# Softmax-minus-one-hot over 8192 x 8192 logits: six in-place f32 row buffers, a row maximum, one compare-and-subtract pass, labels loaded once

## The chip, the cores and the metric

One core of one Trainium2 chip runs the program. The metric is device time in microseconds (us); lower is better. Most executions of one kernel agree within 0.3%. The profile also gives a span, from the first to the last instruction of the program on the core, which is here about 2 us shorter than the time.

In the profile DVE is VectorE, ACT is ScalarE, POOL is GpSimd, PE is TensorE, and SP is the engine that here only issues loads. "ACTq" and "SPq" are the sequencers of ACT and SP issuing a DMA. L85 is line 85 of the kernel.

## The reference

```python
batch, seq_len, vocab = 8, 1024, 8192          # logits f32, labels int
logits_max = np.max(logits, axis=-1, keepdims=True)
exp_logits = np.exp(logits - logits_max)
softmax = exp_logits / np.sum(exp_logits, axis=-1, keepdims=True)
one_hot = ...                                  # 1.0 at the label of each row
return (softmax - one_hot).astype(np.float32)
```

Seen from the chip it is 8192 rows of 8192 f32: 268.44 MB must be read and 268.44 MB written. The kernels cut it into 64 tiles of 128 rows, 4 MB each.

## The kernel before

Each tile is loaded by SP, exponentiated by ACT into bf16 (with the row sum as a by-product and no maximum subtracted), finished by three DVE passes, and stored by ACT's queue. Four row buffers (`bufs=4`) are shared by loading, computing and storing. The labels of each tile come by a small load of their own on POOL's queue.

```python
io_pool = ctx.enter_context(tc.tile_pool(name="io", bufs=4))
work_pool = ctx.enter_context(tc.tile_pool(name="work", bufs=2))
...
for ti in range(n_tiles):
    rs = ti * P
    logits_tile = io_pool.tile([P, V], fp32, tag="io")
    nc.sync.dma_start(out=logits_tile[:], in_=logits_nv[rs : rs + P, :])
    labels_tile = stats_pool.tile([P, 1], labels_n.dtype, tag="labels")
    nc.gpsimd.dma_start(out=labels_tile[:], in_=labels_n[rs : rs + P, None])
    ...                                             # cast of the labels to f32
    nc.scalar.activation(out=exp_bf[:], in_=logits_tile[:], func=Exp, ..., accum_out=sum_f32[:])
    nc.vector.reciprocal(out=recip_sum[:], in_=sum_f32[:])
    ohts_bf = logits_tile.bitcast(bf16)[:, :V]
    nc.vector.tensor_scalar(out=ohts_bf, in0=iota_pv[:, :], scalar1=labels_f32[:],
                            scalar2=sum_f32[:], op0=is_equal, op1=mult)          # L74
    nc.vector.tensor_sub(out=exp_bf[:], in0=exp_bf[:], in1=ohts_bf)              # L83
    nc.vector.tensor_scalar_mul(out=logits_tile[:], in0=exp_bf[:], scalar1=recip_sum[:])  # L85
    nc.scalar.dma_start(out=out_nv[rs : rs + P, :], in_=logits_tile[:])          # L87
```

The softmax here doesn't subtract the row's maximum and nothing guards it: scores larger than these inputs give would overflow.

## Time and profile before

| | before |
|---|---|
| time | 1255.14 us (median of 3, 1254.55 to 1255.56) |
| span of the profiled run | 1252.6 us |
| DMA rate, 200 to 1200 us | 433 GB/s at DMA share 1.00 |
| DVE, ACT busy | 58%, 36% |
| period of a tile in the middle | 19.4 us |

The head of the page of the kernel before, with its DMA part. "q1" carries the loads, "q10" the stores, "q0" the small label loads; the share is the time that their packets took, of 16 engines' span:

```profile
span 1252.6 us, 992 instructions
DVE 732.6 (58%) x320; ACT 457.0 (36%) x129; POOL 253.0 (20%) x69
...
q1 hardware_dynamic: 9216, 268.44, 49.8%
q10 hardware_dynamic: 9216, 268.44, 49.6%
q0 software_dynamic: 2048, 0.07, 0.1%
```

The two large queues together fill 99.4% of the DMA engines' time. No compute engine is near that. The kernel is bound by the DMA engines, and the question for any change is what it does to them.

The table of stretches of the kernel before (columns: stretch, its length, busy us and instructions of DVE, ACT and POOL, PE clock, DMA share, GB/s). A packet is booked in whole where it falls, so short stretches can show a little over 1.00:

```profile
800.00:1000.00 200.00, 118.61 (x53) 73.00 (x22) 42.84 (x10) 1.00 1.00 433
...
1228.00:1232.00 4.00, 2.94 (x3) 1.00 (x2) 0.00 (x0) 1.00 1.08 467
1232.00:1236.00 4.00, 3.99 (x1) 0.00 (x0) 0.00 (x0) 1.00 0.51 221
1236.00:1240.00 4.00, 3.98 (x1) 0.00 (x0) 0.00 (x0) 1.00 0.00 0
1240.00:1244.00 4.00, 0.51 (x1) 0.00 (x0) 0.00 (x0) 1.00 0.92 393
```

In the middle, with transfers cut and issued as they are here, there is nothing to gain short of moving fewer bytes. At the end the DMA engines run dry for several us and then start once more. The timeline of the kernel before shows why (start, length, what):

```profile
1221.87 7.03 ACT L61 ACTIVATE exp_bf<-logits_tile 128x8192 bf16<-128x8192 f32 x1 [12.24 <-DMA logits_tile<-in_logits_dram]
1221.92 0.34 ACTq L87 DMA_DIRECT2D out_dram<-logits_tile  x1
...
1229.11 2.41 DVE L74 TENSOR_SCALAR logits_tile<-iota_pv,labels_f,sum_f 128x8192 bf16<-128x8192 int16 x1
1231.56 4.43 DVE L83 TENSOR_TENSOR exp_bf<-exp_bf,logits_tile 128x8192 bf16<-128x8192 bf16 x1
1236.02 4.49 DVE L85 TENSOR_SCALAR logits_tile<-exp_bf,recip_sum 128x8192 f32<-128x8192 bf16 x1
1240.54 0.34 ACTq L87 DMA_DIRECT2D out_dram<-logits_tile  x1
```

The last load lands at 1221.87. The last store is issued 18.7 us later, but what was still queued for storing lasted only about 12 us.

The time to landing of the large transfers, from the DMA part of the page (columns: count, KB each, median us):

```profile
logits_tile<-in_logits_dram SPq DMA_DIRECT2D x64, 4096.0 KB, 27.2
out_dram<-logits_tile ACTq DMA_DIRECT2D x64, 4096.0 KB, 31.3
```

Read it as an account of buffers: a buffer spends 27.2 us loading, about 19 in compute and 31.3 storing, 77.5 us in all, which is four periods of 19.4. Four buffers are all in use, all the time.

### The profile page before, as it was taken

How to read it: one execution, taken by the hardware profiler on the slowest of the kernel's cores; microseconds unless marked ns; L12 is line 12 of the kernel's file. 1: busy time of each engine (PE TensorE's matmuls, PEld its weight loads, DVE VectorE, ACT ScalarE, POOL GpSimd, SP SyncE). 2: the span in 40 equal slices, each digit the busy share in tenths (PEclk: the TensorE clock that was granted, in tenths of full speed). 3: DMA queues.
4: the chain of work that ended last, by engine and by line, in shares of the span. 5: the costliest groups of instructions: out<-in, count | busy, mean ns of one | idle time of the engine just before them, and what ended most of it. 6: DMA issues, size and time to landing. Idle time of an engine off the chain costs nothing.

```text
span 1252.6 us, 992 instructions
## 1 busy us (share of the span) xinstructions
DVE 732.6 (58%) x320; ACT 457.0 (36%) x129; POOL 253.0 (20%) x69
## 2 busy tenths in 40 slices
DVE  3764655746647556465574664755646556465573
ACT  4424244243342433423424334243342432423422
POOL 5322212212122122221221212212222122100000
DMA  9999999999999999999999999999999999999997
GB/s 400 421 435 434 433 428 430 433 436 433 435 430 432 431 433 433 434 434 432 429 432 435 431 434 433 431 432 432 434 433 434 433 429 432 432 434 435 434 433 311
DMA packets 20487, 537.01 MB, mean 429 GB/s; under 512 B 4096, under 2 KB 4096, under 8 KB 4096
## 3 DMA queue, kind: packets, MB, share of 16 engines
q1 hardware_dynamic: 9216, 268.44, 49.8%
q10 hardware_dynamic: 9216, 268.44, 49.6%
q0 software_dynamic: 2048, 0.07, 0.1%
q14 instruction: 7, 0.06, 0.0%
HBM read 268.50 MB, written 268.44 MB: 429 GB/s over the span
## 4 chain that ended last, share of the span: by engine, by line
DMA 71%; DVE 17%; issue 8%; ACT 1%; POOL 1%; ACTq 0%; SPq 0%; PEldq 0%
DMA out_dram<-logits_tile 38%; DMA logits_tile<-in_logits_dram 32%; DVE logits_tile L85 7%; DVE exp_bf L83 7%; DVE logits_tile L74 4%; ACT exp_bf L61 1%; DMA labels_tile<-in_labels_dram 1%; POOL iota_pv L41 1%; ACTq L87 0%; POOL labels_tile L50 0%; DVE labels_f L57 0%; DVE recip_sum L71 0%; SPq L47 0%; ACTq L61 0%; PEldq L113 0%
## 5 line engine op out<-in xcount | busy, mean ns | idle before, releaser
L61 ACT ACTIVATE exp_bf<-logits_tile 128x8192 bf16<-128x8192 f32 x64 | 449.8, 7029 | 771.3 <-DMA logits_tile<-in_logits_dram 757.8
L50 POOL DMA_DIRECT2D labels_tile<-in_labels_dram x64 | 245.9, 3843 | 832.1 <-DVE labels_f L57 830.1
L71 DVE RECIPROCAL recip_sum<-sum_f 128x1 f32<-128x1 f32 x64 | 10.5, 163 | 485.1 <-ACT exp_bf L61 485.1
L85 DVE TENSOR_SCALAR logits_tile<-exp_bf,recip_sum 128x8192 f32<-128x8192 bf16 x64 | 287.1, 4486 | 0.1
L83 DVE TENSOR_TENSOR exp_bf<-exp_bf,logits_tile 128x8192 bf16<-128x8192 bf16 x64 | 283.2, 4425 | 2.2
L74 DVE TENSOR_SCALAR logits_tile<-iota_pv,labels_f,sum_f 128x8192 bf16<-128x8192 int16 x64 | 154.3, 2412 | 0.3 <-issue 0.3
L57 DVE CAST labels_f<-labels_tile 128x1 f32<-128x1 int32 x64 | 9.4, 147 | 20.2 <-DMA labels_tile<-in_labels_dram 20.2
L61 ACT ACTIVATION_READ_ACCUMULATOR exp_bf<-logits_tile 128x1 f32 x64 | 11.9, 186 | 0.0
L41 POOL IOTA iota_pv<- 128x8192 int16 x1 | 6.9, 6944 | 0.4 <-PEq L113 0.4
L61 ACT ACT_TABLE_LOAD x1 | 1.3, 1283 | 0.7 <-PEq L102 0.7
L102 POOL MEMSET const-float32-0.0<- 128x1 f32 x1 | 0.1, 99 | 0.2 <-issue 0.2
L102 POOL MEMSET const-bfloat16-1.0<- 128x1 bf16 x1 | 0.1, 102 | 0.0
L102 POOL MEMSET const-uint8-127<- 128x1 uint8 x1 | 0.1, 102 | 0.0
L102 POOL MEMSET const-float32-1.0<- 128x1 f32 x1 | 0.1, 99 | 0.0
## 6 DMA issues: line engine op xcount, KB each, us to landing
logits_tile<-in_logits_dram SPq DMA_DIRECT2D x64, 4096.0 KB, 27.2
out_dram<-logits_tile ACTq DMA_DIRECT2D x64, 4096.0 KB, 31.3
labels_tile<-in_labels_dram POOLq DMA_DIRECT2D x64, 1.0 KB, 12.7
```

Of the source, the lines that this page charges most:

```text
L41: nc.gpsimd.iota(iota_pv[:, :], [[1, V]], channel_multiplier=0)
L50: nc.gpsimd.dma_start(out=labels_tile[:], in_=labels_n[rs : rs + P, None])
L57: nc.vector.tensor_copy(out=labels_f32[:], in_=labels_i32)
L61: nc.scalar.activation(out=exp_bf[:], in_=logits_tile[:], func=mybir.ActivationFunctionType.Exp, bias=0.0, scale=1.0, accum_out=sum_f32[:],)
L71: nc.vector.reciprocal(out=recip_sum[:], in_=sum_f32[:])
L74: nc.vector.tensor_scalar(out=ohts_bf, in0=iota_pv[:, :], scalar1=labels_f32[:], scalar2=sum_f32[:], op0=mybir.AluOpType.is_equal, op1=myb ...
L83: nc.vector.tensor_sub(out=exp_bf[:], in0=exp_bf[:], in1=ohts_bf)
L85: nc.vector.tensor_scalar_mul(out=logits_tile[:], in0=exp_bf[:], scalar1=recip_sum[:])
L102: nc = _bacc.Bacc("TRN2", target_bir_lowering=False, num_devices=1)
```

## The change

The intent is exactness (the maximum is subtracted and everything stays f32) without a price. The data stay in place in one f32 buffer per tile, which frees the bf16 buffers and gives six row buffers instead of four. DVE finds the row maximum of tile t+1 while ACT normalizes tile t; one DVE pass per half row compares an index row with the label and subtracts. The labels are loaded once, transposed on PE, and kept. The instructions stay in the order in which they are written.

```diff
-    io_pool = ctx.enter_context(tc.tile_pool(name="io", bufs=4))
-    work_pool = ctx.enter_context(tc.tile_pool(name="work", bufs=2))
+    io = ctx.enter_context(tc.tile_pool(name="io", bufs=SLOTS))      # SLOTS = 6, HALF = 4096
+    ctx.enter_context(tc.manual_schedule())
...
-        nc.gpsimd.dma_start(out=labels_tile[:], in_=labels_n[rs : rs + P, None])
+    nc.scalar.dma_start(out=lab_raw[:], in_=lab_tp)                  # once; then PE transpose
...
+    def row_max(x):
+        nc.vector.tensor_reduce(out=m[:], in_=x[:], axis=X, op=Alu.max, negate=True)
+    def exponent(x, m):
+        nc.scalar.activation(out=x[:], in_=x[:], func=Act.Exp, bias=m[:], scale=1.0, accum_out=s[:])
+    def normalize(x, r):        # two halves
+            nc.scalar.activation(out=xc, in_=xc, func=Act.Copy, bias=0.0, scale=r[:])
+    def subtract(t, x):         # two halves
+            nc.vector.scalar_tensor_tensor(out=xc, in0=iota[:], scalar=lab[:, c, t : t + 1], in1=xc,
+                op0=Alu.is_equal, op1=Alu.subtract, reverse1=True)
...
+    for t in range(T):
+        s = exponent(xs[t], ms[t])
+        r = inverse(s)
+        if t + 1 < T:
+            xs[t + 1] = load(t + 1)
+            ms[t + 1] = row_max(xs[t + 1])
+        if t > 0:
+            store(t - 1, xs[t - 1])
+        normalize(xs[t], r)
+        subtract(t, xs[t])
+    store(T - 1, xs[T - 1])
```

More of the change, by code (lines that the diff above doesn't have):

```diff
@@ L5 @@
 import concourse.tile as tile
-from concourse import bass_utils, mybir
+from concourse import mybir
 from concourse._compat import with_exitstack
 P = 128
+HALF = 4096
+SLOTS = 6
 @with_exitstack
@@ L21 @@
     fp32 = mybir.dt.float32
-    bf16 = mybir.dt.bfloat16
+    i32 = mybir.dt.int32
     i16 = mybir.dt.int16
-    logits_nv = logits.flatten_outer_dims()
-    out_nv = out.flatten_outer_dims()
-    labels_n = labels
-    while len(labels_n.shape) > 1:
-        labels_n = labels_n.rearrange("a b ... -> (a b) ...")
-    N, V = logits_nv.shape
-    assert N % P == 0, f"N={N} must be a multiple of {P}"
-    n_tiles = N // P
-    const_pool = ctx.enter_context(tc.tile_pool(name="const", bufs=1))
-    io_pool = ctx.enter_context(tc.tile_pool(name="io", bufs=4))
@@ L37 @@
-    work_pool = ctx.enter_context(tc.tile_pool(name="work", bufs=2))
-    stats_pool = ctx.enter_context(tc.tile_pool(name="stats", bufs=4))
-    iota_pv = const_pool.tile([P, V], i16)
-    nc.gpsimd.iota(iota_pv[:, :], [[1, V]], channel_multiplier=0)
-    for ti in range(n_tiles):
-        rs = ti * P
-        logits_tile = io_pool.tile([P, V], fp32, tag="io")
-        nc.sync.dma_start(out=logits_tile[:], in_=logits_nv[rs : rs + P, :])
-        labels_tile = stats_pool.tile([P, 1], labels_n.dtype, tag="labels")
-        nc.gpsimd.dma_start(out=labels_tile[:], in_=labels_n[rs : rs + P, None])
-        labels_f32 = stats_pool.tile([P, 1], fp32, tag="labels_f32")
-        if mybir.dt.size(labels_n.dtype) == 8:
-            labels_i32 = labels_tile.bitcast(mybir.dt.int32)[:, :1]
-        else:
-            labels_i32 = labels_tile[:]
-        nc.vector.tensor_copy(out=labels_f32[:], in_=labels_i32)
-        exp_bf = work_pool.tile([P, V], bf16, tag="exp")
-        sum_f32 = stats_pool.tile([P, 1], fp32, tag="sum")
-        nc.scalar.activation(
-            out=exp_bf[:],
-            in_=logits_tile[:],
-            func=mybir.ActivationFunctionType.Exp,
-            bias=0.0,
-            scale=1.0,
-            accum_out=sum_f32[:],
-        )
-        recip_sum = stats_pool.tile([P, 1], fp32, tag="recip")
-        nc.vector.reciprocal(out=recip_sum[:], in_=sum_f32[:])
-        ohts_bf = logits_tile.bitcast(bf16)[:, :V]
-        nc.vector.tensor_scalar(
-            out=ohts_bf,
-            in0=iota_pv[:, :],
-            scalar1=labels_f32[:],
-            scalar2=sum_f32[:],
-            op0=mybir.AluOpType.is_equal,
-            op1=mybir.AluOpType.mult,
-        )
-        nc.vector.tensor_sub(out=exp_bf[:], in0=exp_bf[:], in1=ohts_bf)
-        nc.vector.tensor_scalar_mul(out=logits_tile[:], in0=exp_bf[:], scalar1=recip_sum[:])
-        nc.scalar.dma_start(out=out_nv[rs : rs + P, :], in_=logits_tile[:])
@@ new lines @@
+    Act = mybir.ActivationFunctionType
+    Alu = mybir.AluOpType
+    x_nv = logits.flatten_outer_dims()
+    o_nv = out.flatten_outer_dims()
+    N, V = x_nv.shape
+    T = N // P
+    C = V // HALF
+    lab_tp = labels.rearrange("a b -> (a b)").rearrange("(t p) -> t p", p=P)
+    const = ctx.enter_context(tc.tile_pool(name="const", bufs=1))
+    io = ctx.enter_context(tc.tile_pool(name="io", bufs=SLOTS))
+    stats = ctx.enter_context(tc.tile_pool(name="stats", bufs=4))
+    psum = ctx.enter_context(tc.tile_pool(name="psum", bufs=1, space=bass.MemoryType.PSUM))
@@ new lines @@
+    ctx.enter_context(tc.manual_schedule())
+    lab_raw = const.tile([T, P], labels.dtype)
+    nc.scalar.dma_start(out=lab_raw[:], in_=lab_tp)
+    iota = const.tile([P, HALF], i16)
+    nc.gpsimd.iota(iota[:], [[1, HALF]], base=0, channel_multiplier=0)
+    ident = const.tile([T, T], fp32)
+    nc.gpsimd.memset(ident[:], 0.0)
+    nc.gpsimd.affine_select(
+        out=ident[:], in_=ident[:], compare_op=Alu.not_equal, fill=1.0,
+        base=0, pattern=[[-1, T]], channel_multiplier=1,
+    )
@@ new lines, with load @@
+    lab_f = const.tile([T, P], fp32)
+    lab32 = lab_raw[:].bitcast(i32)
+    step = mybir.dt.size(labels.dtype) // 4
+    nc.vector.tensor_copy(out=lab_f[:], in_=lab32.rearrange("t (p s) -> t p s", s=step)[:, :, 0])
+    lab_ps = psum.tile([P, T], fp32)
+    nc.tensor.transpose(out=lab_ps[:], in_=lab_f[:], identity=ident[:])
+    lab = const.tile([P, C, T], fp32)
+    for c in range(C):
+        nc.vector.tensor_scalar_add(out=lab[:, c, :], in0=lab_ps[:], scalar1=float(-c * HALF))
+    def load(t):
+        x = io.tile([P, V], fp32, tag="x", name="x")
+        nc.sync.dma_start(out=x[:], in_=x_nv[t * P : (t + 1) * P, :])
+        return x
@@ new lines, in row_max, with inverse @@
+    def row_max(x):
+        m = stats.tile([P, 1], fp32, tag="m", name="m")
+        nc.vector.tensor_reduce(out=m[:], in_=x[:], axis=mybir.AxisListType.X, op=Alu.max, negate=True)
+        return m
+    def exponent(x, m):
+        s = stats.tile([P, 1], fp32, tag="s", name="s")
+        nc.scalar.activation(out=x[:], in_=x[:], func=Act.Exp, bias=m[:], scale=1.0, accum_out=s[:])
+        return s
+    def inverse(s):
+        r = stats.tile([P, 1], fp32, tag="r", name="r")
+        nc.vector.reciprocal(out=r[:], in_=s[:])
+        return r
@@ new lines, in normalize, with store @@
+    def normalize(x, r):
+        for c in range(C):
+            xc = x[:, c * HALF : (c + 1) * HALF]
+            nc.scalar.activation(out=xc, in_=xc, func=Act.Copy, bias=0.0, scale=r[:])
+    def subtract(t, x):
+        for c in range(C):
+            xc = x[:, c * HALF : (c + 1) * HALF]
+            nc.vector.scalar_tensor_tensor(
+                out=xc, in0=iota[:], scalar=lab[:, c, t : t + 1], in1=xc,
+                op0=Alu.is_equal, op1=Alu.subtract, reverse1=True,
+            )
+    def store(t, x):
+        nc.scalar.dma_start(out=o_nv[t * P : (t + 1) * P, :], in_=x[:])
@@ L91 @@
+    xs, ms = {}, {}
+    xs[0] = load(0)
+    ms[0] = row_max(xs[0])
+    for t in range(T):
[9 more added lines that the diff above has]
+    store(T - 1, xs[T - 1])
 _INS = ['logits', 'labels']
```

## The prediction

> **What bounds it now.** The DMA engines, not the compute. The page's head gives 537.01 MB and 429 GB/s; the two big queues hold 49.8% and 49.6% of 16 engines' span. The table of stretches shows DMA share 1.00 and 433 GB/s from 200 to 1200 us, while DVE is busy 58% and ACT 36%. One 4 MB load plus one 4 MB store take 8.39 MB / 433 GB/s = 19.4 us, and the timeline shows that period between exponentials. Compute lines in the chain of waits are links between transfers, not the limit: DVE needs 11.5 us per tile, ACT 7.2. The Trainium skill, "SBUF — State Buffer", The DMA setup-cost knee, gives 436 GB/s as the asymptote of 16 ports; 433 agrees, so the steady rate has nothing left. What is left is at the ends: in the stretches after 1230 us the DMA share falls to 0 (about 1234 to 1240.5), because the last store waits for exponential and three DVE passes; about 6.5 us lost.
>
> **What the change does, per tile of 19.4 us.**
> - Bytes of loads and stores: unchanged.
> - Removed: 2.4 + 4.4 + 4.5 us of 16-bit or two-port DVE passes; 64 label loads (q0, 0.1% of the span, about 1 us) and their casts.
> - Added on DVE: a row maximum over 8192 f32 elements and two compare-subtract passes over 4096. The skill, "VectorE: DVE Perf Modes", The perf-mode tier table, has tensor_reduce and f32 tensor_tensor at one element per cycle; it has no entry for the compare-subtract instruction, which I take as tensor_tensor. The trace's bf16 tensor_tensor, two per cycle, takes 4.43 us for 8192, so twice that: about 8.6 us maximum, 2 x 4.35 us subtract. DVE about 17.4 us per tile (estimate), 1115 us in all.
> - Added on ACT: a normalizing pass, estimated from the 7.03 us exponential as 2 x 3.6 us. ACT about 14.5 us per tile, one table load.
> - The dependency cycle: maximum of t+1 stands before subtract of t on DVE, so the store of t follows the landing of t+1 by about 17.4 us. Cycle about 17.5 us, under 19.4: hidden, with 2 us to spare.
> - Slots: before, 27.2 us load landing + 31.3 store landing + 19 compute = 77.5 = 4 periods. After, a slot spends about 37 us in compute, and 6 periods are 116 us, so about 80 us stay for transfers: loads near 30 us to landing as before, stores near 45 to 50. Both queues stay full.
>
> **Critical path.** Steady state unchanged: same bytes, same rate. Head: same, perhaps 1 us more in the loads-only phase. Tail: last load to last store grows from 18.7 to about 30 us, but the store backlog at that moment grows from about 1.25 to about 2.5 tiles, plus one store issued 17 us later: about 34 us of DMA work, so the 6.5 us gap closes. Label traffic saves about 1 us.
>
> **Predicted: 1248 us**, 1242 to 1258 in 8 of 10. Faster by over 2%: 0.01; within 2%: 0.95; slower: 0.04.
>
> **What would show it.** DMA share 1.00 and 432 to 434 GB/s in the middle; DVE about 88% busy, ACT about 72%; maximum about 8.6 us, each subtract about 4.4; DVE's main wait before the maximum, for the load; median store landing 45 us or more; no zero-DMA stretch before the last store. Wrong steps: a reduced steady rate; a tail gap that persists or widens; stores landing near 31 us (backlog did not build).
>
> **What would make it wrong.** The compare-subtract with int16 and f32 inputs running at half my rate (DVE 26 us per tile, 1650 us); waits between ACT and DVE that push the cycle over 19.4 us; a tail with the stores drained before the last one is ready (+5 to 15 us).

## The result, and the profile after

The changed kernel took 1248.47 us (median of 4, 1247.99 to 1248.57) against 1254.86 us of the kernel before (median of 4, partly the runs above). Ratios here are the mean time of one kernel's fast runs over that of the other's of the same rounds, so not quite the ratio of the medians quoted: 0.9948, with a 95% interval of 0.9934 to 0.9962. That is 0.5% faster.

The head and DMA part of the page of the changed kernel:

```profile
span 1246.1 us, 997 instructions
PE 0.3 (0%) x1; PEld 0.2 (0%) x1; DVE 1122.1 (90%) x259; ACT 930.7 (75%) x257; POOL 4.1 (0%) x7
...
q1 hardware_dynamic: 9216, 268.44, 50.0%
q10 hardware_dynamic: 9296, 268.51, 49.9%
```

Both compute engines work far more than before and the kernel is still bound by DMA, now 99.9% of the span. This is what "off the critical path" looks like: about 390 us of DVE time and 474 us of ACT time were added, and the span fell by 6.5 us.

The groups of instructions of the changed kernel (after the bar: total us, mean ns of one; then idle time before them and what ended it):

```profile
L70 DVE TENSOR_REDUCE m<-x 128x1 f32<-128x8192 f32 x64 | 555.7, 8683 | 83.8 <-DMA x<-in_logits_dram 83.7
L75 ACT ACTIVATE x<-x,m 128x8192 f32<-128x8192 f32 x64 | 455.8, 7122 | 157.0 <-DVE m L70 157.0
L91 DVE SCALAR_TENSOR_TENSOR x<-iota,lab,x 128x4096 f32<-128x4096 int16 x128 | 567.9, 4479 | 4.1 <-ACT x L86 4.1
L86 ACT ACTIVATE x<-x,r 128x4096 f32<-128x4096 f32 x128 | 467.7, 3700 | 123.5 <-DVE r L80 123.5
```

DVE's only real idle time is 83.7 us before the row maximum, in front of a load. That is the slack that DVE has left, about 1.8 us in each period of 19.4 once the loads have become the limit. The Trainium skill ("VectorE: DVE Perf Modes", The perf-mode tier table) has tensor_reduce at one element per cycle whatever the type. With the clock of 0.96 GHz from the page's Specifications that is an estimate of 8533 ns for 8192 elements; the measured 8683 ns agrees. The two ACT passes use two functions and the page lists one ACT_TABLE_LOAD, which agrees with "ScalarE: Activation LUTs", Table sets, where cheap functions such as copy come with every set.

The stretches of the changed kernel that answer to those shown of before (columns as above, with PE and its weight load in front):

```profile
800.00:1000.00 200.00, 0.00 (x0) 0.00 (x0) 181.49 (x43) 150.54 (x41) 0.00 (x0) 1.00 1.00 433
...
1226.00:1230.00 4.00, 0.00 (x0) 0.00 (x0) 3.94 (x1) 0.00 (x0) 0.00 (x0) 1.00 0.95 410
1230.00:1234.00 4.00, 0.00 (x0) 0.00 (x0) 0.00 (x0) 0.00 (x0) 0.00 (x0) 1.00 0.97 418
1234.00:1238.00 4.00, 0.00 (x0) 0.00 (x0) 0.00 (x0) 0.00 (x0) 0.00 (x0) 1.00 1.12 483
1238.00:1242.00 4.00, 0.00 (x0) 0.00 (x0) 0.00 (x0) 0.00 (x0) 0.00 (x0) 1.00 0.95 410
1242.00:1246.10 4.10, 0.00 (x0) 0.00 (x0) 0.00 (x0) 0.00 (x0) 0.00 (x0) 1.00 0.09 40
```

The middle is the same 433 GB/s. The empty stretch before the last store is gone: the DMA engines stay full until about 1242 us, while compute ended at about 1230. The timeline of the changed kernel around its last store:

```profile
1199.43 8.69 DVE L70 TENSOR_REDUCE m<-x 128x1 f32<-128x8192 f32 x1 [1.81 <-DMA x<-in_logits_dram]
...
1221.06 8.88 DVE L91 SCALAR_TENSOR_TENSOR x<-iota,lab,x 128x4096 f32<-128x4096 int16 x2 [4.08 <-ACT x L86]
1229.97 0.34 ACTq L97 DMA_DIRECT2D out_dram<-x  x1
```

From the last load's landing to the last store's issue it is now 30.5 us, 12 us more than before. It costs nothing because more stores are queued at that moment, which the landing times show:

```profile
x<-in_logits_dram SPq DMA_DIRECT2D x64, 4096.0 KB, 24.2
out_dram<-x ACTq DMA_DIRECT2D x64, 4096.0 KB, 55.0
```

A store issued every 19.4 us that takes 55.0 us to land means 2.8 stores in flight; before it was 31.3 / 19.4 = 1.6.

One caution about the chain of waits of the changed kernel: it gives "another core or an unknown queue 66%". There is one core only. The chain lost track at SP's waits for finished stores. The DMA shares and the waits, not this chain, name the limit.

### The profile page after: what moved, and what is told of

The parts are those of the page before. It is cut to its first block, busy times and chain, and to the rows that moved or that the text cites. A ratio compares the mean times of both kernels' runs of the same rounds, so it can differ in the third digit from the quotient of the medians.

```text
span 1246.1 us, 997 instructions
## 1 busy us (share of the span) xinstructions
PE 0.3 (0%) x1; PEld 0.2 (0%) x1; DVE 1122.1 (90%) x259; ACT 930.7 (75%) x257; POOL 4.1 (0%) x7
## 4 chain that ended last, share of the span: by engine, by line
another core or an unknown queue 66%; DVE 21%; DMA 7%; issue 3%; SPq 1%; ACT 1%; DVEq 0%; ACTq 0%
DVE m L70 11%; DVE x L91 10%; DMA out_dram<-x 4%; DMA x<-in_logits_dram 3%; SPq L65 1%; ACT x L75 1%; DVEq L139 0%; ACT x L86 0%; DVE r L80 0%; ACTq L97 0%; DVEq L91 0%; DVEq L70 0%
## 5 line engine op out<-in xcount | busy, mean ns | idle before, releaser
L70 DVE TENSOR_REDUCE m<-x 128x1 f32<-128x8192 f32 x64 | 555.7, 8683 | 83.8 <-DMA x<-in_logits_dram 83.7
L75 ACT ACTIVATE x<-x,m 128x8192 f32<-128x8192 f32 x64 | 455.8, 7122 | 157.0 <-DVE m L70 157.0
L91 DVE SCALAR_TENSOR_TENSOR x<-iota,lab,x 128x4096 f32<-128x4096 int16 x128 | 567.9, 4479 | 4.1 <-ACT x L86 4.1
L86 ACT ACTIVATE x<-x,r 128x4096 f32<-128x4096 f32 x128 | 467.7, 3700 | 123.5 <-DVE r L80 123.5
L80 DVE RECIPROCAL r<-s 128x1 f32<-128x1 f32 x64 | 10.2, 159 | 7.3 <-ACT x L75 7.3
L75 ACT ACTIVATION_READ_ACCUMULATOR x<-x,m 128x1 f32 x64 | 12.0, 187 | 0.0
L75 ACT ACT_TABLE_LOAD x1 | 1.3, 1283 | 13.4 <-DMA x<-in_logits_dram 13.4
L46 POOL IOTA iota<- 128x4096 int16 x1 | 3.5, 3542 | 0.4 <-POOLq L128 0.4
## 6 DMA issues: line engine op xcount, KB each, us to landing
x<-in_logits_dram SPq DMA_DIRECT2D x64, 4096.0 KB, 24.2
```

What stands on the lines that cost most here:

```text
L46: nc.gpsimd.iota(iota[:], [[1, HALF]], base=0, channel_multiplier=0)
L70: nc.vector.tensor_reduce(out=m[:], in_=x[:], axis=mybir.AxisListType.X, op=Alu.max, negate=True)
L75: nc.scalar.activation(out=x[:], in_=x[:], func=Act.Exp, bias=m[:], scale=1.0, accum_out=s[:])
L80: nc.vector.reciprocal(out=r[:], in_=s[:])
L86: nc.scalar.activation(out=xc, in_=xc, func=Act.Copy, bias=0.0, scale=r[:])
L91: nc.vector.scalar_tensor_tensor(out=xc, in0=iota[:], scalar=lab[:, c, t : t + 1], in1=xc, op0=Alu.is_equal, op1=Alu.subtract, reverse1=True,)
```

## The experiments

The theory is the "ends theory": both kernels are bound by the same DMA traffic at the same rate, and the 6.4 us came from the end (no idle DMA stretch, thanks to a deeper queue of stores) and from the 64 small label loads. Rivals: that the label loads are nearly all of it, that the steady state improved, or that something else in the rewritten compute helped. Each of the nine timed kernels ran against the kernel before in the same rounds; where a ratio is turned into us here, it is (1 - ratio) x 1255. Experiments 1, 2, 3 and the floor shared one set of runs of the kernel before (median 1255.7 us), 5, 6, 8 and 9 another (1254.94 us); 4 had its own (1254.77 us). The rounds ran on different chips of the same kind, each beside the kernel before. "Packet records" are the single DMA packets that the trace keeps; what is counted from them here is in no view of the profile.

### 1. The labels alone, in the kernel before

```diff
-        nc.gpsimd.dma_start(out=labels_tile[:], in_=labels_n[rs : rs + P, None])   # and its cast
+    nc.scalar.dma_start(out=lab_raw[:], in_=labels_n.rearrange("(t p) -> t p", p=P))   # once, then PE transpose
-            scalar1=labels_f32[:],
+            scalar1=lab[:, ti : ti + 1],
```

> The kernel before, with the labels loaded and transposed once as in the changed kernel; nothing else. Ends theory (about 5 us of the 6.4 us saved is the idle DMA stretch before the last store, about 1.3 us is the traffic of 64 small label loads): 1253.5 us, that is 1.3 us faster than before, and the idle DMA stretch before the last store stays about 6.5 us. Rival, labels theory (the 64 label loads cost most of what was saved, by disturbing the big transfers): 1249 to 1250 us.

Measured: 1252.68 us, ratio 0.9977 (0.9965 to 0.9989), that is 2.9 us. The idle stretch stayed; in the stretches of this kernel the DMA share falls just as before (columns: stretch, length, PE, PE weight load, DVE, ACT, POOL, PE clock, DMA share, GB/s):

```profile
1232.00:1236.00 4.00, 0.00 (x0) 0.00 (x0) 3.96 (x2) 0.00 (x0) 0.00 (x0) 1.00 0.15 66
1236.00:1240.00 4.00, 0.00 (x0) 0.00 (x0) 2.83 (x1) 0.00 (x0) 0.00 (x0) 1.00 0.30 131
```

The labels are worth something, but not nearly all of the 6.4 us, so the labels theory falls. How much is less sure: the timed runs differ by 2.9 us with an interval from 1.4 to 4.4, the profiled spans by 1.7 us (1252.6 and 1250.9). By the packet records of the kernel before, the packets of the label loads took 1.5 us of the 16 engines' time; the 0.1% of the page is rounded.

### 2. The tail alone, in the kernel before: split the last tile's passes and its store in four

```diff
+        parts = 4 if ti == n_tiles - 1 else 1
+        w = V // parts
+        for c in reversed(range(parts)):
+            cs = slice(c * w, (c + 1) * w)
-        nc.vector.tensor_sub(out=exp_bf[:], in0=exp_bf[:], in1=ohts_bf)
+            nc.vector.tensor_sub(out=exp_bf[:, cs], in0=exp_bf[:, cs], in1=ohts_bf[:, cs])
...                                     # multiply and store likewise, piece by piece
```

> The kernel before, with the last two passes and the store of the last tile alone in four column pieces, each stored as soon as it is done. Ends theory: the first piece of the last store is issued about 13 us after the last load lands instead of 18.7, the idle DMA stretch shrinks from 6.5 us to 1 to 3 us, and the kernel gains 4 to 6 us: 1249 to 1251 us. Labels theory or a theory of a better steady rate: no change, 1255 us.

Measured: 1251.2 us, ratio 0.9965 (0.9953 to 0.9977), that is 4.4 us (2.9 to 5.9; the profiled spans differ by 3.2). The stretch is shorter but not gone (DMA share 0.46 from 1232 to 1236 us and 0.66 from 1236 to 1240), as expected for a first piece issued 13.3 us after the last landing. Sixty-three tiles of this kernel are as before, so the gain lies in the end.

### 3. Five buffers in the kernel before, as the scheduler ordered it

```diff
-    io_pool = ctx.enter_context(tc.tile_pool(name="io", bufs=4))
+    io_pool = ctx.enter_context(tc.tile_pool(name="io", bufs=5))
-    iota_pv = const_pool.tile([P, V], i16)
+    iota_pv = const_pool.tile([P, H], i16)          # H = V // 2, compared in two halves, to make room
```

> The kernel before with five row buffers instead of four (the index row is halved to make room, so the compare is done in two halves and one tiny DVE pass per tile is added; the labels are still loaded 64 times). Ends theory: median store landing rises from 31 to about 50 us, one more store (9.7 us of DMA work) is queued when the last load lands, the idle stretch before the last store is gone: 1248.5 to 1250 us. Labels theory: 1255 us.

Measured: 1253.84 us, ratio 0.9998 (0.9975 to 1.002). A miss. (One of its six runs, at 1263.69 us, stands out and widens the interval; without it the mean is 1.8 us below that of the kernel before, still far from the range expected.) Median store landing was 33.7 us, not 50, so the queue had not deepened; the timeline of this kernel says why:

```profile
1184.91 0.19 ACT L62 ACTIVATION_READ_ACCUMULATOR exp_bf<-logits_tile 128x1 f32 x1
1185.21 1.35 DVE L78 TENSOR_SCALAR logits_tile<-iota_pv,labels_f,sum_f 128x4096 bf16<-128x4096 int16 x1
1186.47 4.48 DVE L90 TENSOR_SCALAR logits_tile<-exp_bf,recip_sum 128x8192 f32<-128x8192 bf16 x1
...
1190.98 10.58 ACTq L92 DMA_DIRECT2D out_dram<-logits_tile  x2
```

In every second tile the scheduler had put the last pass (L90) behind the first compare of the next tile, and that compare waits for the next tile's exponential. A finished tile waited for its neighbour, stores went out in pairs, and the added buffer was spent on waiting. Adding a buffer is not the same as adding depth to the queue: the order decides who holds it.

### 4. Five buffers again, in program order

Five buffers and the halved index row as in experiment 3, and:

```diff
+    ctx.enter_context(tc.manual_schedule())
...
+        if done is not None:
+            nc.scalar.dma_start(out=done[0], in_=done[1])     # store of the tile before, behind this exponential
...
-        nc.scalar.dma_start(out=out_nv[rs : rs + P, :], in_=logits_tile[:])
+        done = (out_nv[rs : rs + P, :], logits_tile[:])
```

> Five row buffers in the kernel before once more, now with the instructions in program order (each store right behind the next tile's exponential; the compare of a tile never ahead of the multiply of the tile before), because the scheduler had answered the fifth buffer by issuing stores in pairs. Ends theory: median store landing about 50 us, no idle stretch before the last store, 1249 to 1251 us with the label loads still there. If a fifth buffer does not help the tail of this kernel: 1254 us or more, store landing still near 31 us.

Measured: 1250.89 us, ratio 0.9969 (0.9955 to 0.9982), that is 3.9 us. The store line of its page's DMA part, and then its last stretches, read:

```profile
out_dram<-logits_tile ACTq DMA_DIRECT2D x64, 4096.0 KB, 46.1
```

```profile
1232.00:1236.00 4.00, 2.49 (x1) 0.00 (x0) 0.00 (x0) 1.00 0.89 385
1236.00:1240.00 4.00, 0.00 (x0) 0.00 (x0) 0.00 (x0) 1.00 0.96 410
1240.00:1244.00 4.00, 0.00 (x0) 0.00 (x0) 0.00 (x0) 1.00 1.10 475
```

The stretch is closed with the label loads still in place. A deeper store queue does it, without the changed kernel's compute. This kernel changes the order as well as the buffers, and its four-buffer twin was not run; the landing times of the kernel before and of experiments 3 and 4 (31.3, 33.7, 46.1 us), and the stores still queued when the last load has landed (counted below), are what ties the gain to depth rather than to order as such.

### 5. Both halves together: labels once and the split tail, in the kernel before

The edits of experiments 1 and 2, both:

```diff
-            scalar1=labels_f32[:],
+            scalar1=lab[:, ti : ti + 1],
...
+        parts = 4 if ti == n_tiles - 1 else 1
```

> The kernel before with labels once and the last tile's store split. Ends theory: both parts add up, 1248 to 1249.5 us, level with the changed kernel, with none of its other changes. If something else in the changed kernel saves time: 1251 us or more.

Measured: 1248.72 us, ratio 0.9952 (0.9937 to 0.9967), beside 0.9948 for the changed kernel. The two edits of experiments 1 and 2, with none of the rest, bring the kernel before level with the changed kernel. Their single gains, 2.9 and 4.4 us, add to 7.3 where 6.0 was measured, which lies inside their intervals. No other part of the change is needed to explain the time.

### 6. The label loads put back into the changed kernel, unused

```diff
+        nc.gpsimd.dma_start(out=junk[:], in_=flat[t * P : (t + 1) * P, None])
+        nc.vector.tensor_copy(out=junk_f[:], in_=junk[:].bitcast(i32)[:, :1])
```

> The changed kernel with the 64 small label loads and their casts put back (unused). Ends theory: 1 to 1.5 us slower than the changed kernel, 1249.7 us. Labels theory: 5 us slower, 1253 us or more.

Measured: 1251.29 us, ratio to the kernel before 0.9969 against the changed kernel's 0.9948, so 2.6 us slower; again more than expected and again not most of the gain. (The two ratios come from different rounds and their intervals overlap, but each of the four runs of one kernel is at least 2.6 us from each of the other's.) The packets of the label loads took 1.6 us here by the packet records, so about 1 us is not the packets' own time. In the packet records of this run the 16 engines ended their last store over 3.9 us (1244.0 to 1247.9 us), in the changed kernel over 2.5 us (1242.4 to 1244.9). It may be that the label loads leave the engines more unevenly loaded and that the last one is waited for; that this accounts for the rest was not tested.

### 7. The floor: loads and stores only

```diff
     for t in range(T):
         x = io.tile([P, V], fp32, tag="x", name="x")
         nc.sync.dma_start(out=x[:], in_=x_nv[t * P : (t + 1) * P, :])
-        ...                                     # all compute
         nc.scalar.dma_start(out=o_nv[t * P : (t + 1) * P, :], in_=x[:])
```

> Only the 64 loads and 64 stores, six buffers, no compute; wrong result on purpose. It is the floor of this traffic. Ends theory: the changed kernel sits on it, so 1246.5 to 1248.5 us. A theory that the changed kernel still loses time in its steady state: 1240 us or less.

Its output is wrong, which doesn't matter for the time. Measured: 1247.18 us, ratio 0.9933 (0.992 to 0.9946). The changed kernel at 0.9948 lies within 2 us of a program that computes nothing at all. So there is next to nothing left in it to gain with this traffic. Whether the same bytes in transfers of another size or order would have a lower floor was not tried.

### 8. The changed kernel with five buffers

```diff
-SLOTS = 6
+SLOTS = 5
```

> The changed kernel with five row buffers instead of six. Slot account: five periods of 19.4 us are 97 us; 37 us in compute and 24 us of load leave about 36 us for a store. Store backlog when the last load lands falls from about 2.8 to about 1.9 stores, and the DMA idles about 5 us in the tail: 1252 to 1254 us, with the middle still at 433 GB/s. If the number of buffers is not the cause: 1248.4 us.

Measured: 1258.63 us, ratio 1.0027 (1.0012 to 1.0042). The direction and the store landing (35.6 us) are as expected, the size is not: 10 us instead of 5. Its stretches show two holes in the tail:

```profile
800.00:1200.00 400.00, 0.00 (x0) 0.00 (x0) 361.13 (x83) 300.12 (x84) 0.00 (x0) 1.00 1.00 433
...
1226.00:1232.00 6.00, 0.00 (x0) 0.00 (x0) 4.65 (x3) 4.05 (x3) 0.00 (x0) 1.00 0.27 115
1232.00:1238.00 6.00, 0.00 (x0) 0.00 (x0) 3.26 (x1) 6.00 (x2) 0.00 (x0) 1.00 1.02 437
1238.00:1244.00 6.00, 0.00 (x0) 0.00 (x0) 5.62 (x2) 0.31 (x1) 0.00 (x0) 1.00 0.41 175
```

The DMA idles 4.4 us before the second-last store (6.00 x 0.73) and 3.5 us before the last. In all, the packet records show the 16 engines idle for 9.9 us against 2.1 in the changed kernel; the profiled spans differ by 9.5. I had expected one hole of about 5 us, and had left out that a store needs about 1 us from issue until its packets run (issued 1243.65; the packet records show no engine busy at 1244.0 and all 16 at 1245.0). With five buffers the changed compute is slower than the kernel before; the sixth buffer is what pays for its longer path.

### 9. The changed kernel with four buffers

```diff
-SLOTS = 6
+SLOTS = 4
```

> The changed kernel with four row buffers, as many as before. Four periods are 77.5 us, less 37 us compute leaves 41 us for a load and a store, which need about 21 us each at half rate: the queues just run dry. Slot account: steady period 19.4 to 20 us and about 14 us idle in the tail: 1265 to 1290 us. If buffers are not the cause: 1248.4 us.

Measured: 1322.78 us, ratio 1.0529 (1.0485 to 1.0574), slower than the whole range expected. Now the middle suffers too: 414 to 416 GB/s from 200 to 1200 us, loads and stores landing after 22.2 and 21.8 us, so about 20.2 us per tile (8.39 MB / 415 GB/s). The DMA share in that stretch is 0.99, so the engines count as busy 99% of the time and yet move 4% less than 433 GB/s. The packet records show where this goes. In the changed kernel over 99% of the load packets of 32 KB between 200 and 1200 us took 1.21 us; here 11% of them took more than 1.25 us, some over 2 us, and 94% of the added time fell in the first 6 us after a load was issued. The first 16 packets of the run's very first load took 1.6 to 2.2 us too. It looks as if, with only four buffers, the load queue runs empty and each new load starts slowly; that was not tested.

### 10. How much slack DVE has: two sizes of extra work

```diff
+        nc.vector.tensor_reduce(out=junk[:], in_=x[:, :1024], axis=X, op=Alu.max)   # and with 4096
```

> The changed kernel with one more DVE maximum per tile, over 1024 elements (about 1.15 us, result unused). DVE's cycle rises from 17.4 to about 18.6 us, under the 19.4 us of the transfers: hidden, 1248 to 1250 us. If DVE is what bounds the changed kernel: 64 x 1.15 = 74 us more, 1322 us.

> The same over 4096 elements (about 4.35 us). DVE's cycle becomes 21.8 us, over 19.4: DVE bounds, 13 us head + 64 x 21.8 + about 30 us tail: 1420 to 1445 us.

Measured, one run each (state unknown; the kernel before, run beside them once, took 1254.68 us): 1249.56 us and 1432.49 us, both as expected. The groups of the two kernels, the one with 1024 first, show where the added time went:

```profile
L70 DVE TENSOR_REDUCE m<-x 128x1 f32<-128x8192 f32 x64 | 555.0, 8672 | 16.8 <-DMA x<-in_logits_dram 16.7
L72 DVE TENSOR_REDUCE junk<-x 128x1 f32<-128x1024 f32 x64 | 77.2, 1206 | 0.0
```

```profile
L70 DVE TENSOR_REDUCE m<-x 128x1 f32<-128x8192 f32 x64 | 554.5, 8665 | 0.1
L72 DVE TENSOR_REDUCE junk<-x 128x1 f32<-128x4096 f32 x64 | 282.0, 4406 | 0.0
```

In the first, 77.2 us of new DVE work cost about 1 us, because DVE's wait for loads shrank from 83.7 to 16.7 us. In the second the wait is gone, DVE bounds, and the time rises by 184 us. The idle time in front of the row maximum is a true measure of slack.

### 11. The order of the two DVE passes

```diff
-            ms[t + 1] = row_max(xs[t + 1])      # ahead of subtract(t)
         normalize(xs[t], r)
         subtract(t, xs[t])
+            ms[t + 1] = row_max(xs[t + 1])      # behind it
```

> The changed kernel with the subtract of tile t ahead of the maximum of tile t+1 on DVE. Same work, but each engine now waits for the other: 7.3 exponential + 3.9 first half of normalizing + 8.9 subtract + 8.7 maximum + 0.3 = 29 us per tile, over 19.4: 1850 to 1900 us. If only the sum of each engine's work counted (DVE 17.4 us): 1248 us.

Measured, one run (state unknown): 1863.94 us. The same instructions, and DVE is busy 61% only. Its waits:

```profile
ACT x L75 <- DVE m L70: 886.0, 64, 14.0
DVE r L80 <- ACT x L75: 466.0, 64, 7.3
DVE x L91 <- ACT x L86: 241.7, 64, 3.9
```

Each engine waits for the other in turn. The sum of an engine's work is a lower bound; the cycle through both engines is what must fit under the 19.4 us of the transfers.

## Why the prediction was right

- **The time.** Predicted 1248 us; measured 1248.47. The 433 GB/s of the middle did not change, and experiment 7 shows that the changed kernel is within 2 us of the floor of this traffic. The packet records of the two profiled runs (spans 6.4 us apart) give the same account: the 16 engines idled 7.1 us in the kernel before and 2.1 us in the changed one, and the packets of the label loads had taken 1.5 us.
- **The compute costs.** Predicted DVE 17.4 us per tile; measured 8.68 + 2 x 4.48 = 17.6. Predicted ACT 14.5; measured 7.12 + 2 x 3.70 + 0.19 = 14.7. Doubling the bf16 pass of the trace was a good estimate for the f32 passes. That they fit under 19.4 us only in this order is shown by experiment 11, and that less than 2 us of room is left by experiment 10.
- **The tail.** The closing of the gap was right and its cause, more queued stores, is shown from both sides: experiment 4 with more of them, experiment 8 with fewer (experiment 2 shows only what the gap costs). The packet records let the queue be counted: the stores issued but not yet moved at the end of the last load, in tiles, times 9.7 us per tile (4.19 MB / 433 GB/s), against the time until the next store was issued:

  | | tiles queued | lasts (us) | next store issued after (us) | queue ran dry |
  |---|---|---|---|---|
  | before | 1.3 | 12.6 | 19.2 | yes |
  | experiment 3 | 0.8 | 8.0 | 13.4 | yes |
  | experiment 4 | 2.0 | 19.6 | 19.4 | just not |
  | experiment 8 | 1.4 | 13.9 | 18.0 | yes |
  | changed | 2.5 | 24.4 | 18.0 | no |

  The prediction had put about 1.25 tiles before and about 2.5 after. The gain was not the whole 6.5 us: experiment 2, which only narrowed the gap, gained 4.4 (2.9 to 5.9), and the idle time of the changed kernel fell by 5.0. Part is given back because its engines end their last store over 2.5 us, where those of the kernel before, all started afresh after the gap, ended within 0.2 us.
- **The labels.** Mis-sized: put at about 1 us, measured at 2.9 us (1.4 to 4.4) taken out of the kernel before and 2.6 put into the changed one. The packets' own time is 1.5 to 1.6 us; the rest had no term in the sum and stays open. The tail was put too high and the labels too low, and the two errors nearly cancelled: 7.1 us predicted below 1255.14, 6.4 measured. That the sum came within 0.5 us is in part luck.
- **The landing times.** The sum was right (80 us predicted, 24.2 + 55.0 = 79.2 measured), the split was not: loads were put near 30 and stores at 45 to 50. The extra depth all went to the store queue, and even a little of the load queue's.

## What to carry to other kernels

When the DMA engines are full in the middle, look at the two ends: here the time left at the end was set by how many transfers were still queued when the last load landed, against how long the last tiles computed. Count a buffer's life in periods (landing + compute + landing = buffers x period) before adding or removing one; what compute takes is taken from the queue. Work may be added freely to an engine up to the idle time in front of its loads, as long as the cycle through all engines, and not only each sum, stays under the transfers' period.

## What the Trainium skill lacked or had wrong

- "SBUF — State Buffer", Summary, says to estimate HBM transfers at about 358 GB/s, and "DMA: Bandwidth & Descriptors", Where 436 GB/s comes from, has the HBM side bind there. Here one core alone moved 433 GB/s between HBM and SBUF for 1.2 ms, loads and stores mixed, close to the 436 GB/s that the first page gives for the SBUF ports. So the rule of 358 does not fit a core that runs alone; "HBM Reference", Specifications, says that a core alone measures about 425 and that 358 is its share when both cores of a pair stream, which is much nearer.
- "VectorE: DVE Perf Modes", The perf-mode tier table, has no entry for scalar_tensor_tensor, and no other page gives a time for it. With int16 and f32 inputs and an f32 output, 128x4096 took 4.48 us, which is one element per cycle of 0.96 GHz plus about 0.2 us.
- "DMA: Bandwidth & Descriptors", Why small descriptors are slow, gives the overhead of a small descriptor itself, but no page says what small loads cost the large transfers that run beside them. Sixty-four 1 KB label loads cost 2.6 to 2.9 us by the point values (interval of the latter 1.4 to 4.4), of which their packets' time is 1.5 to 1.6 us.
- The skill warns in general words that the busy share of the DMA engines can mislead, but no page says by how much: a DMA share of 0.99 went with 415 GB/s in the four-buffer kernel, against 433 GB/s at 1.00, where 11% of the load packets took over 1.25 us instead of the usual 1.21.
